# A two-layer mixer trunk: casts of weights behind the heads' high parts, numerators of two heads back to back, head 0's low part on VectorE, and a SwiGLU that starts with 256 features of gate and up in one bank

## The chip, the cores and the metric

The kernel runs on one core of one Trainium2 chip. The metric is device time in microseconds (us) of one execution. TensorE is called PE, VectorE DVE, ScalarE ACT, GpSimd POOL, and SyncE, which issues the loads, SP. L153 is line 153 of the kernel; the changed kernel is some lines shorter, so its L152 is the same line.

## The reference

The input is 256 tokens of 1024 features. Two layers follow each other, each with a token mixer, a SwiGLU channel mixer and a gated embedding:

```python
for i in range(2):
    y = gmlp_mixer(x, ...) if i == 0 else mlstm_mixer(x, ...)
    x = layer_norm(ALPHA * x + y, ln1_g[i], ln1_b[i])
    x = layer_norm(ALPHA * x + swiglu(x, ffn_w_gate[i], ffn_w_up[i], ffn_w_down[i]), ln2_g[i], ln2_b[i])
    gate = sigmoid(x @ ple_w_gate[i] + ple_b_gate[i])
    x = x + gate * (p[i] @ ple_w_proj[i])

def swiglu(x, w_gate, w_up, w_down):          # 2816 features = 22 blocks of 128
    return (silu(x @ w_gate) * (x @ w_up)) @ w_down
```

The mLSTM mixer of layer 1 has four heads of 512 features. A head's score matrix, times a decay, gives a numerator (scores times values) and a denominator (row sums); the quotient is normalised per head, a skip term is added, the result is multiplied by silu(z) and projected down. Everything is float32.

## The kernel before

**Arithmetic.** Each float32 operand of a matmul is split into a high part (a cast to fp32r, on ACT) and a low part (a subtraction, on DVE; `split`, L153). A product is three matmuls: high by high, low by high, high by low.

**Weights.** Weights arrive as float32 tiles of 128 x 1024 (512 KB) into four raw buffers through SP's queue, in the order of `weight_plan`; `EARLY` moves some of them ahead in that order, and those of `WIDE` live in a pool of large tiles of their own ("b8"). `weight(...)` is called where a tile is used and keeps up to 8 tiles loaded and up to 4 split ahead of the use. A raw buffer is free again, and the next load can start, when the tile's cast and its subtraction are done. `behind["cast"]` names instructions after which the casts called for from then on are put in the order. A scheduler sets the order of each engine's instructions from dependencies and program order; ACT's order in the heads follows the program.

**PSUM.** Matmul results go to eight banks, four in pool A (accumulators, heads' numerators) and four in pool B.

**SwiGLU** (`channel_mixer`). The tokens are two tiles of 128. First, `first(t)` computes 512 features of gate and then 512 of up for tile t with the tokens stationary: 8 chunks of 128 inputs times three products, 24 matmuls of 512 columns each for gate and for up (L286 and L287 high and low weights, L289 the input's low part). That makes 96 matmuls for both tiles. Between gate and up of tile 0 stands `transpose_x(1)` (L326), which turns token tile 1 of the normalised input (xn) into feature-major order, splits it and so makes tile 1's part of xs. The layer norm before it runs on DVE (L335 to L344). The products silu(gate) times up (hn) are token-major; four PE transposes per tile (L562) turn them into the first four feature blocks. The other 18 blocks come from `gate_up(f)`, which keeps the weights stationary: for gate and up each 8 matmuls of 512 columns (L260, the high and low part of xs side by side) and 8 of 256 (L264). The down projection (`Down`, L240 to L242) takes 12 matmuls of 512 columns per feature block and runs two blocks behind.

**Heads** (`mlstm`). For each head, DVE adds a mask to gate sums (gm, L909), ACT takes three exponentials (e, L911 to L913), DVE multiplies the scores by them (sc, L917), ACT casts the high part (phi, L153), and POOL subtracts the low part (plo, L153). Meanwhile PE computes blocks of z (zps, 24 matmuls of 256 columns, L245 to L247). `pv_block(h)` then computes head h's numerators for both token tiles (num, L937 to L939, two banks of pool A) and denominators (pd, L943 and L944). DVE takes the statistics (dn to hrs, L949 to L961), POOL a power (L962), DVE the factors (hrs and nb, L963 and L965), and ACT writes the normalised rows (hn, L967), which frees the two banks. `h_block(h)` transposes hn on PE (L976), and DVE and ACT finish and split the four feature blocks of the head (y, L980, L981; h, L153). Afterwards `acc = Down(NI)` takes the four banks of pool A for the down projection. The order before, on PE, is: numerators of head 0, z block 12, head 1, z 13, head 2, z 14, transposes of head 0, head 3, z 15, transposes of head 1, accumulation.

Of the kernel before, what the change touches and what calls it, by code (L numbers as in the profile page):

```python
# [14 lines left out]
P = 128  # L15
D = 1024
S = 256
# [29 lines left out]

WIDE = {(n, l, k) for l in range(2) for n, m in (("g", 4), ("u", 2), ("pg", 6)) for k in range(m)}  # L50
EARLY = {("wo", 17 + k): ("g", 0, k) for k in range(4)}
EARLY |= {("mo", 8 + 2 * k): ("g", 1, k) for k in range(3)}
EARLY |= {("d", l, 10 + k): ("pg", l, k) for l in range(2) for k in range(6)}


def down_blocks(f):

    return range(4) if f == 3 + LAG else [f - LAG] if f > 3 + LAG else []

# [2 lines left out]

def stationary(key):

    return key[0] in ("u", "xm") and len(key) == 2 or key[0] in ("g", "u", "z") and key[-1] >= 4


def paired(key):  # L70

    return key[0] in ("g", "u") and len(key) == 3 and key[-1] >= 4 or key[0] == "u" and len(key) == 2


def weight_plan(a):
# [3 lines left out]
    def add(key, ap):  # L79
        plan.append((key, ap))  # L80
# [11 lines left out]

    def ffn(l):
        add(("pj", l, 0), a["ple_proj"][l, 0])
        for n in ("g", "u"):
            for kp in range(4):
                add((n, l, kp), a["ffn_" + n][l, kp])
        for f in range(4, NF + LAG):
            for n in ("g", "u") if f < NF else ():
                add((n, l, f), a["ffn_" + n][l, f])  # L100
            for e in down_blocks(f):
                add(("d", l, e), a["ffn_d"][l, e])
        add(("pj", l, 1), a["ple_proj"][l, 1])
        for k in range(KD):
            add(("pg", l, k), a["ple_gate"][l, k])
# [28 lines left out]
def trunk(ctx, tc, a, out):  # L134
# [10 lines left out]
    def tl(tag, shape, dt=F32, name="t"):  # L145
        return sb.tile(shape, dt, tag=tag, name=name, bufs=BUFS[tag])

    def bank(which, shape, name="ps"):
        return (psA if which == "A" else psB).tile(shape, F32, tag=which, name=name)
# [58 lines left out]
    def weight(*key, casts=None):  # L208
        at["use"] = max(at["use"], place[key])
        ahead(LOAD_AHEAD, CAST_AHEAD if casts is None else casts)  # L210
        at["use"] = max(at["use"], place[key] + 1)
        return wt.pop(place[key])
# [304 lines left out]
    def channel_mixer(l, acc, last, hook=None):  # L517
# [19 lines left out]

        fw = {}  # L540

        def first(t, between=lambda: None):
            ps = {}
            for n in ("g", "u"):
                if t == 0:
                    fw[n] = [weight(n, l, kp) for kp in range(4)]
                ps[n] = bank("B", [P, 512], "first")
                tok_from_x(ps[n], t, fw[n])
                if n == "g":
                    between()  # L550
            h = tl("m2", [P, 512], name="hn")
            act.activation(h, ps["g"], AF.Silu)
            dve.tensor_tensor(h, h, ps["u"], ALU.mult)
            return h

        hn = [first(0, lambda: transpose_x(1)), first(1)]
        hs = {e: tl("h", [P, 2, S], F32R, "h") for e in range(4)}

        def transpose_h(t):
            tp = bank("B", [P, 4, P], "tp")  # L560
            for e in range(4):
                pe.transpose(tp[:, e, :], hn[t][:, e * P:(e + 1) * P], ident)  # L562
            for e in range(4):
                split(hs[e][:, 0, TOK[t]], hs[e][:, 1, TOK[t]], tp[:, e, :])

        def gate_up(f):
# [20 lines left out]

        transpose_h(0)
        rows = []
        for f in range(4, NF + LAG):  # L590
            if f < NF:
                gate_up(f)
            if f == 4:
                transpose_h(1)
                acc = Down(NF)
            for e in down_blocks(f):
                acc.add(e, hs.pop(e), weight("d", l, e, casts=1 if f >= NF else None))
            if f in (8, 10, 12):

                with issue_after([at["dma"]]):  # L600
                    rows.append(load_row(a[("ln2_g", "ln2_b", "ple_b")[f // 2 - 4]][l]))
            if f == 14 and hook:
                hook()
            if f == NF - 1:
                ahead(LOAD_AHEAD, LAG + 1)
# [96 lines left out]
    def mlstm(embed1):  # L702
# [156 lines left out]
        with tc.manual_schedule(engines={mybir.EngineType.Activation}):  # L859
# [43 lines left out]
            for h in range(NH):  # L903
# [13 lines left out]
                dve.scalar_tensor_tensor(p, p, DH ** -0.5, e, ALU.mult, ALU.mult)  # L917
                hi = tl("h", [P, 384], F32R, "phi")
                lo = tl("h", [P, 384], F32R, "plo")
                split(hi, lo, p, sub=pool)  # L920
                ph.append((hi, lo))
            z_copy(*z)
            act.activation(sz[1][:, 0:4, :], sz[1][:, 0:4, :], AF.Silu)

# [58 lines left out]
                    split(hs[f][:, 0, :], hs[f][:, 1, :], y)  # L983

        for h in range(NH):
            if h == NH - 1:
                ahead(LOAD_AHEAD, 4)
            pv_block(h)
            z_act(*z_mm(12 + h))
            if h == NH - 2:  # L990
                h_block(0)
        acc = Down(NI)
        begin = []
        for h in range(NH):
# [21 lines left out]
def lay_out(inputs):  # L1016
# [26 lines left out]
    def part(w):  # L1043
# [11 lines left out]
        "gm_wsT": i["gm_w_s"][0].transpose(2, 0, 1).reshape(P, NG * P),  # L1055
        "gm_bs": i["gm_b_s"][0].reshape(-1),
        "gm_gb": np.stack([i["gm_ln_g"][0], i["gm_ln_b"][0]], 1).reshape(NU, P, 2).transpose(1, 0, 2),
        "ffn_g": np.stack([mixed(w) for w in i["ffn_w_gate"]]),
        "ffn_u": np.stack([mixed(w) for w in i["ffn_w_up"]]),
        "ffn_d": i["ffn_w_down"].reshape(2, NF, P, D),  # L1060
        "ple_proj": i["ple_w_proj"].reshape(2, 2, P, 2, 512).transpose(0, 3, 2, 1, 4).reshape(2, 2, P, D),
        "ple_gate": i["ple_w_gate"].reshape(2, KD, P, D),
# [41 lines left out]
```

## Time and profile before

| what | value |
| --- | --- |
| median of 3 runs | 825.27 us (825.23 to 825.81) |
| profiled execution | 825.63 us |
| its span | 823.9 us |
| PE busy | 816.9 us, 99% of the span, 4520 matmuls |
| DVE busy | 614.3 us, 75% |
| ACT busy | 470.9 us, 57% |
| POOL busy | 149.6 us, 18% |
| granted clock of PE | 1.0 |
| data moved | 155.52 MB, mean 189 GB/s |

A row of a timeline gives the start in us, the duration in us, engine, line, operation, output and inputs by the program's names, and how many like it follow each other. In brackets stands the idle time of the engine before it and what ended that. Matmuls are pipelined: the duration of one reaches over the start of the next, so PE's time for one is read from start to start. The span leaves out 1.7 us around the profiled execution.

### The profile page before, as it was taken

What the parts mean: (1) busy time and instruction counts of PE and PEld (TensorE: products, weight loads), DVE (VectorE), ACT (ScalarE), POOL (GpSimd) and SP (SyncE); (2) the same over time, 40 slices, a digit from 0 to 9 for tenths busy, and PEclk for the clock granted to TensorE, in tenths of its full rate; (3) what the DMA queues carried; (4) which work ended last, traced back from release to release, by engine and by line L of the source; (5) the groups of instructions that cost most, each with busy time, mean ns of one, the idle gap of its engine ahead of it and who ended that gap; (6) DMA issues with size and microseconds to landing.
All of it is one profiled execution on the core that took longest, in us unless ns stands there. A gap on an engine that the chain in (4) does not pass through costs nothing.

```text
span 823.9 us, 12407 instructions
## 1 busy us (share of the span) xinstructions
PE 816.9 (99%) x4520; PEld 708.0 (86%) x4520; DVE 614.3 (75%) x982; ACT 470.9 (57%) x820; POOL 149.6 (18%) x209
## 2 busy tenths in 40 slices
PE   9999999999999999999999999999999999999997
PEld 6888888888888888888889999988888888888886
DVE  6757998678956567586878998889885656776674
ACT  6656666565535556475256788776444555665522
POOL 1020643342000000700001677330000000000000
PEclk9999999999999999999999999999999999999999
DMA  8895447567176678677144355454626667886501
GB/s 287 283 337 182 153 159 225 179 194 243 67 260 202 192 225 281 201 229 252 38 146 156 135 162 161 146 177 147 215 90 224 196 199 228 269 264 212 179 1 51
DMA packets 44997, 155.52 MB, mean 189 GB/s; under 512 B 5256, under 2 KB 6024, under 8 KB 44936
## 3 DMA queue, kind: packets, MB, share of 16 engines
q1 hardware_dynamic: 44792, 154.60, 57.6%
q8 instruction: 35, 0.57, 0.3%
q14 instruction: 26, 0.21, 0.1%
q10 hardware_dynamic: 144, 0.13, 0.0%
HBM read 153.67 MB, written 1.05 MB: 188 GB/s over the span
## 4 chain that ended last, share of the span: by engine, by line
PE 96%; DVE 1%; ACT 1%; DMA 1%; issue 0%; POOL 0%; SPq 0%; DVEq 0%; ACTq 0%
PE acc L240 9%; PE acc L241 9%; PE acc L242 9%; PE pu L260 8%; PE pg L260 8%; PE ups L260 5%; PE pg L264 4%; PE pu L264 4%; PE ups L264 3%; PE vps L242 2%; PE vps L240 2%; PE vps L241 2%; PE xmps L245 2%; PE xmps L247 2%; PE xmps L246 2%; PE gate L289 2%
## 5 line engine op out<-in xcount | busy, mean ns | idle before, releaser
L153 DVE TENSOR_TENSOR w<-raw,w 128x1024 fp32r<-128x1024 f32 (+1 forms) x275 | 333.2, 1219 | 74.7 <-ACT w L153 73.1
L153 ACT CAST w<-raw 128x1024 fp32r<-128x1024 f32 (+1 forms) x275 | 284.9, 1046 | 120.6 <-PE acc L242 25.7
L240 PE MATMUL acc<-w,h 128*128 128x512 f32 x336 | 133.0, 396 | 0.2 <-ACT hn L967 0.2
L241 PE MATMUL acc<-w,h 128*128 128x512 f32 x336 | 131.3, 391 | 0.0
L242 PE MATMUL acc<-w,h 128*128 128x512 f32 x336 | 131.0, 390 | 0.0
L242 PEld LDWEIGHTS acc<-w,h 128*128 128x128 f32 x336 | 63.1, 188 | 13.9
L240 PEld LDWEIGHTS acc<-w,h 128*128 128x128 f32 x336 | 63.1, 188 | 12.1 <-ACT hn L967 0.6
L241 PEld LDWEIGHTS acc<-w,h 128*128 128x128 f32 x336 | 63.1, 188 | 11.2 <-DVE h L153 0.2
L260 PE MATMUL pg<-xs,w 128*128 128x512 f32 x288 | 71.6, 391 | 0.0
L260 PE MATMUL pu<-xs,w 128*128 128x512 f32 x288 | 71.5, 390 | 0.0
L260 PEld LDWEIGHTS pg<-xs,w 128*128 128x128 f32 x288 | 53.8, 188 | 11.0
L260 PEld LDWEIGHTS pu<-xs,w 128*128 128x128 f32 x288 | 53.8, 188 | 11.0
L319 POOL TENSOR_TENSOR rs<-ve,mhalf 128x1 f32<-128x1 f32 x8 | 7.6, 956 | 295.9 <-DVE ve L318 291.3
L271 ACT COPY s<-pg 128x256 f32<-128x256 f32 x36 | 13.4, 372 | 69.7 <-PE pg L264 69.7
L260 PE MATMUL ups<-xs,w 128*128 128x512 f32 x192 | 47.9, 391 | 0.0
L272 DVE TENSOR_TENSOR s<-s,pg 128x256 f32<-128x256 f32 x36 | 15.1, 421 | 42.8 <-ACT s L271 42.7
L260 PEld LDWEIGHTS ups<-xs,w 128*128 128x128 f32 x192 | 35.7, 188 | 7.2
L264 PEld LDWEIGHTS pg<-xs,w 128*128 128x128 f32 x288 | 38.9, 188 | 3.1
L264 PE MATMUL pg<-xs,w 128*128 128x256 f32 x288 | 39.5, 280 | 0.0
L264 PE MATMUL pu<-xs,w 128*128 128x256 f32 x288 | 39.4, 279 | 0.0
L264 PEld LDWEIGHTS pu<-xs,w 128*128 128x128 f32 x288 | 36.5, 188 | 0.3
L245 PE MATMUL xmps<-xs,w 128*128 128x256 f32 x128 | 36.3, 284 | 0.0
(252 smaller groups left out, 1635.7 us busy)
## 6 DMA issues: line engine op xcount, KB each, us to landing
raw<-in_ffn_g SPq DMA_DIRECT2D x44, 512.0 KB, 4.4
raw<-in_ffn_u SPq DMA_DIRECT2D x44, 512.0 KB, 4.6
raw<-in_ffn_d SPq DMA_DIRECT2D x44, 512.0 KB, 4.3
raw<-in_gm_u SPq DMA_DIRECT2D x24, 512.0 KB, 3.5
raw<-in_gm_wo SPq DMA_DIRECT2D x24, 512.0 KB, 3.4
raw<-in_gm_v SPq DMA_DIRECT2D x21, 512.0 KB, 5.2
raw<-in_ple_gate SPq DMA_DIRECT2D x16, 512.0 KB, 4.5
raw<-in_ml_z SPq DMA_DIRECT2D x16, 512.0 KB, 3.8
```

What stands on the lines that cost most here:

```text
L153: return dve.tensor_copy(hi, src) if fast else act.copy(hi, src), sub.tensor_tensor(lo, src, hi.bitcast(F32), ALU.subtract)
L240: pe.matmul(ps, lh, w[:, 0, c], start=start, stop=False)
L241: pe.matmul(ps, ll, w[:, 0, c], start=False, stop=False)
L242: pe.matmul(ps, lh, w[:, 1, c], start=False, stop=stop)
L245: pe.matmul(ps, w[:, 0, c], h, start=start, stop=False)
L246: pe.matmul(ps, w[:, 0, c], l, start=False, stop=False)
L247: pe.matmul(ps, w[:, 1, c], h, start=False, stop=stop)
L260: pe.matmul(ps, w[:, 0, k * P:(k + 1) * P], xs[:, k], start=k == 0, stop=False)
L264: pe.matmul(ps[:, 0], w[:, 1, k * P:(k + 1) * P], xh[:, k, :], start=False, stop=k == KD - 1)
L271: act.copy(o, ps[:, 1])
L272: dve.tensor_tensor(o, o, ps[:, 0], ALU.add)
L289: pe.matmul(ps, xl[:, k, TOK[t]], w[:, 0, c], start=False, stop=k == KD - 1)
```

## The change

There are four edits.

1. **SwiGLU.** `first(t)` now computes 256 features of gate and the same 256 of up side by side in one bank of 512 columns, from four weight tiles "f" that hold both: 24 matmuls per token tile, 48 in all. The loop over `gate_up` starts at feature block 2 and makes 20 blocks. `transpose_x(1)` stands in tile 0 after the 16 matmuls with the input's high part. Two transposes per tile turn hn, which has 256 columns. In each layer 44 weight tiles are read, as before.
2. **Weights ahead.** The four "f" tiles of each layer are moved ahead and live in large tiles (before: four gate tiles in layer 0 and three in layer 1 were moved ahead, and four gate and two up tiles of each layer were in large tiles).
3. **Casts behind the high parts.** After the last head's high part is cast, `behind["cast"]` names that cast, so casts of weights called for later stand behind it. Head 0's low part is subtracted on DVE, those of the others on POOL as before.
4. **Heads in pairs.** The order on PE is: numerators of head 0, z 12, head 1, z 13, head 2, head 3, z 14, transposes of head 0, z 15, transposes of head 1, accumulation. The call that looks ahead in the weights moves behind the transposes of head 0.

```diff
-WIDE = {(n, l, k) for l in range(2) for n, m in (("g", 4), ("u", 2), ("pg", 6)) for k in range(m)}
-EARLY = {("wo", 17 + k): ("g", 0, k) for k in range(4)}
-EARLY |= {("mo", 8 + 2 * k): ("g", 1, k) for k in range(3)}
+WIDE = {(n, l, k) for l in range(2) for n, m in (("f", 4), ("pg", 6)) for k in range(m)}
+EARLY = {("wo", 17 + k): ("f", 0, k) for k in range(4)}
+EARLY |= {("mo", 8 + 2 * k): ("f", 1, k) for k in range(4)}
...
-    return range(4) if f == 3 + LAG else [f - LAG] if f > 3 + LAG else []
+    return range(2) if f == 1 + LAG else [f - LAG] if f > 1 + LAG else []
...
-        for n in ("g", "u"):
-            for kp in range(4):
-                add((n, l, kp), a["ffn_" + n][l, kp])
-        for f in range(4, NF + LAG):
+        for kp in range(4):
+            add(("f", l, kp), a["ffn_f"][l, kp])
+        for f in range(2, NF + LAG):
...
+        def first(t, before=(None, None)):
+            if t == 0:
+                fw.extend(weight("f", l, kp) for kp in range(4))
+            ps = bank("B", [P, 512], "first")
+            tok_from_x(ps, t, fw, before)
+            h = tl("m2", [P, 256], name="hn")
+            act.activation(h, ps[:, :256], AF.Silu)
+            dve.tensor_tensor(h, h, ps[:, 256:], ALU.mult)
             return h
-        hn = [first(0, lambda: transpose_x(1)), first(1)]
-        hs = {e: tl("h", [P, 2, S], F32R, "h") for e in range(4)}
+        hn = [first(0, (0, lambda: transpose_x(1))), first(1)]
+        hs = {e: tl("h", [P, 2, S], F32R, "h") for e in range(2)}
...
-        for f in range(4, NF + LAG):
+        for f in range(2, NF + LAG):
             if f < NF:
                 gate_up(f)
-            if f == 4:
+            if f == 2:
                 transpose_h(1)
...
-                split(hi, lo, p, sub=pool)
+                end = split(hi, lo, p, sub=pool if h else dve)
                 ph.append((hi, lo))
+            behind["cast"] = end[:1]
...
         for h in range(NH):
-            if h == NH - 1:
-                ahead(LOAD_AHEAD, 4)
             pv_block(h)
-            z_act(*z_mm(12 + h))
-            if h == NH - 2:
-                h_block(0)
+            if h < 2:
+                z_act(*z_mm(12 + h))
+        z_act(*z_mm(14))
+        h_block(0)
+        ahead(LOAD_AHEAD, 4)
+        z_act(*z_mm(15))
```

The order of instructions shows what the edits move. On PE at the first features of layer 0, the rows before around the transposes of token tile 1 (xn_80):

```order
741 L286 MATMUL first<-w,xs 128x512
742 L287 MATMUL first<-w,xs 128x512
743 L289 MATMUL first<-w,xs 128x512 x8
744 L326 MATMUL tp<-ident,xn_80 128x128 x8
745 L286 MATMUL first<-w,xs 128x512
```

and now:

```order
741 L285 MATMUL first<-w,xs 128x512
742 L286 MATMUL first<-w,xs 128x512
743 L325 MATMUL tp<-ident,xn_80 128x128 x8
744 L288 MATMUL first<-w,xs 128x512 x8
745 L285 MATMUL first<-w,xs 128x512
```

The eight transposes stood behind tile 0's 24 gate matmuls and stand now behind its first 16; row 745 began tile 0's up features and now begins tile 1.

On ACT in the heads, from head 1's last exponential to the switch of the function table, the rows before:

```order
486 L913 ACTIVATE e<-gm,cols 128x128
487 L915 ACTIVATE cols<-cols 128x8
488 L153 CAST w<-raw 128x1024
489 L153 CAST phi<-sc 128x384
490 L911 ACTIVATE e<-gm,cols 128x128
491 L912 ACTIVATE e<-gb,cols 128x128
492 L913 ACTIVATE e<-gm,cols 128x128
493 L153 CAST w<-raw 128x1024
494 L153 CAST phi<-sc 128x384
```

and now, from head 3's high part on:

```order
502 L152 CAST phi<-sc 128x384
503 L749 COPY sz<-zps 128x256
504 L746 ACT_TABLE_LOAD
505 L746 ACTIVATE sz<-zps 128x256
506 L921 ACTIVATE sz<-sz 128x1024
507 L965 ACTIVATE hn<-num,nb,hrs 128x512 x2
508 L152 CAST w<-raw 128x1024
509 L965 ACTIVATE hn<-num,nb,hrs 128x512 x2
510 L746 ACTIVATE sz<-zps 128x256
511 L152 CAST w<-raw 128x1024 x4
512 L746 ACTIVATE sz<-zps 128x256
513 L965 ACTIVATE hn<-num,nb,hrs 128x512 x2
```

The casts of weights between the heads' steps are gone from there; the first comes behind head 0's normalised rows (507), and four stand together between z 13 (510) and z 14 (512), ahead of head 2's rows (513).

On DVE at the same place, the rows before, from the mask additions of the heads to the second product of scores:

```order
562 L909 TENSOR_TENSOR gm<-gb,cmask 128x256 x2
563 L153 TENSOR_TENSOR w<-raw,w 128x1024
564 L917 SCALAR_TENSOR_TENSOR sc<-sc,e 128x384
565 L153 TENSOR_TENSOR w<-raw,w 128x1024
566 L909 TENSOR_TENSOR gm<-gb,cmask 128x256
```

and now, from head 0's on:

```order
569 L904 TENSOR_TENSOR gm<-gb,cmask 128x256 x2
570 L912 SCALAR_TENSOR_TENSOR sc<-sc,e 128x384
571 L904 TENSOR_TENSOR gm<-gb,cmask 128x256
572 L152 TENSOR_TENSOR plo<-sc,phi 128x384
573 L912 SCALAR_TENSOR_TENSOR sc<-sc,e 128x384
```

The subtractions of weights have left the stretch, and head 0's low part stands between the third mask addition and the second product of scores.

More of the change, by code (lines that the diff above doesn't have):

```diff
@@ L45 @@
 Z_AFTER_XM = {1: 4, 5: 5, 10: 6, 15: 7}
-WIDE = {(n, l, k) for l in range(2) for n, m in (("g", 4), ("u", 2), ("pg", 6)) for k in range(m)}
-EARLY = {("wo", 17 + k): ("g", 0, k) for k in range(4)}
-EARLY |= {("mo", 8 + 2 * k): ("g", 1, k) for k in range(3)}
+WIDE = {(n, l, k) for l in range(2) for n, m in (("f", 4), ("pg", 6)) for k in range(m)}
+EARLY = {("wo", 17 + k): ("f", 0, k) for k in range(4)}
+EARLY |= {("mo", 8 + 2 * k): ("f", 1, k) for k in range(4)}
 EARLY |= {("d", l, 10 + k): ("pg", l, k) for l in range(2) for k in range(6)}
 def down_blocks(f):
-    return range(4) if f == 3 + LAG else [f - LAG] if f > 3 + LAG else []
+    return range(2) if f == 1 + LAG else [f - LAG] if f > 1 + LAG else []
 ASIDE = 56
 def stationary(key):
-    return key[0] in ("u", "xm") and len(key) == 2 or key[0] in ("g", "u", "z") and key[-1] >= 4
+    return key[0] in ("g", "u", "xm") or key[0] == "z" and key[-1] >= 4
 def paired(key):
-    return key[0] in ("g", "u") and len(key) == 3 and key[-1] >= 4 or key[0] == "u" and len(key) == 2
+    return key[0] in ("g", "u")
 def weight_plan(a):
@@ L94, in ffn @@
         add(("pj", l, 0), a["ple_proj"][l, 0])
-        for n in ("g", "u"):
-            for kp in range(4):
-                add((n, l, kp), a["ffn_" + n][l, kp])
-        for f in range(4, NF + LAG):
+        for kp in range(4):
+            add(("f", l, kp), a["ffn_f"][l, kp])
+        for f in range(2, NF + LAG):
             for n in ("g", "u") if f < NF else ():
-                add((n, l, f), a["ffn_" + n][l, f])
+                add((n, l, f), a["ffn_" + n][l, f - 2])
             for e in down_blocks(f):
@@ L536, in channel_mixer @@
         boundary(0, g1, b1)
[L540 to L553, printed above, removed]
-            return h
-        hn = [first(0, lambda: transpose_x(1)), first(1)]
-        hs = {e: tl("h", [P, 2, S], F32R, "h") for e in range(4)}
+        fw = []
+        def first(t, before=(None, None)):
[6 more added lines that the diff above has]
+            dve.tensor_tensor(h, h, ps[:, 256:], ALU.mult)
+            return h
+        hn = [first(0, (0, lambda: transpose_x(1))), first(1)]
+        hs = {e: tl("h", [P, 2, S], F32R, "h") for e in range(2)}
         def transpose_h(t):
-            tp = bank("B", [P, 4, P], "tp")
-            for e in range(4):
+            tp = bank("B", [P, 2, P], "tp")
+            for e in range(2):
                 pe.transpose(tp[:, e, :], hn[t][:, e * P:(e + 1) * P], ident)
-            for e in range(4):
+            for e in range(2):
                 split(hs[e][:, 0, TOK[t]], hs[e][:, 1, TOK[t]], tp[:, e, :])
@@ L1057, in lay_out @@
         "gm_gb": np.stack([i["gm_ln_g"][0], i["gm_ln_b"][0]], 1).reshape(NU, P, 2).transpose(1, 0, 2),
-        "ffn_g": np.stack([mixed(w) for w in i["ffn_w_gate"]]),
-        "ffn_u": np.stack([mixed(w) for w in i["ffn_w_up"]]),
+        "ffn_f": np.stack([
+            tok(np.concatenate([g[:, :256], u[:, :256]], 1))[0] for g, u in zip(i["ffn_w_gate"], i["ffn_w_up"])
+        ]),
+        "ffn_g": np.stack([feat(w[:, 256:]) for w in i["ffn_w_gate"]]),
+        "ffn_u": np.stack([feat(w[:, 256:]) for w in i["ffn_w_up"]]),
         "ffn_d": i["ffn_w_down"].reshape(2, NF, P, D),
```

## The prediction

> **What bounds the kernel now.** I read the page first, then the list of waits on TensorE (PE), then the chain that ended last. On the page, busy time and the chain by engine:
>
> ```profile
> PE 816.9 (99%) x4520; PEld 708.0 (86%) x4520; DVE 614.3 (75%) x982; ACT 470.9 (57%) x820; POOL 149.6 (18%) x209
> ...
> PE 96%; DVE 1%; ACT 1%; DMA 1%; issue 0%; POOL 0%; SPq 0%; DVEq 0%; ACTq 0%
> ```
>
> The waits of PE, each group with its total, its count and its longest:
>
> ```profile
> PE warm L357 <- DVE warm L354: 1.2, 1, 1.2
> PE vps L422 <- ACT w L382: 0.6, 1, 0.6
> PE num L939 <- POOL plo L153: 0.5, 1, 0.5
> PE vps L422 <- ACT xs L378: 0.2, 1, 0.2
> PE acc L240 <- ACT hn L967: 0.2, 1, 0.2
> ```
>
> PE is busy for 816.9 of 823.9 us and 96% of the chain is its own work. Behind the start it waits twice in the whole program: for head 0's low part, and for head 3's normalised rows. So time can be won only by fewer or shorter PE instructions and at these two waits, and it can be lost only where another engine, now hidden, becomes later than PE. The profiled execution took 825.63 us, 0.36 above the median of 825.27; I sum changes on it and take them from the median.
>
> **SwiGLU, each layer.** The timeline of PE, from the start of the first features in layer 0 to the first block, and one later turn of the loop:
>
> ```profile
> 219.52 0.39 PE L286 MATMUL first<-w,xs 128*128 128x512 f32 x1
> ...
> 223.15 1.98 PE L289 MATMUL first<-w,xs 128*128 128x512 f32 x8
> 224.97 1.04 PE L326 MATMUL tp<-ident,xn 128*128 128x128 f32 x8
> 225.76 0.47 PE L286 MATMUL first<-w,xs 128*128 128x512 f32 x1
> ...
> 242.21 0.60 PE L562 MATMUL tp<-ident,hn 128*128 128x128 f32 x4
> 242.56 1.18 PE L260 MATMUL pg<-xs,w 128*128 128x512 f32 x4
> ...
> 265.08 1.29 PE L260 MATMUL pg<-xs,w 128*128 128x512 f32 x5
> ...
> 273.32 0.84 PE L260 MATMUL pg<-xs,w 128*128 128x512 f32 x3
> ```
>
> A 512-column matmul takes (223.15 − 219.52)/16 = 0.227 us of PE (0.2275 over the eight from 223.15 to 224.97). The change drops 48 of the 96 matmuls of the first features: 48 × 0.2275 = 10.92 us. It adds two more turns of gate and up. One loop turn is 273.32 − 265.08 = 8.24 us and holds, beside one such block, 12 matmuls of 512 columns for the down projection (2.73), so the block is 5.51; the down matmuls stay as many. A block is 16 matmuls of 512 columns and 16 of 256, and the chain has eight of the latter:
>
> ```profile
> 246.50 0.94 PE pg L264 x8
> ```
>
> That is 0.1175 each, so the widths alone give 16 × 0.2275 + 16 × 0.1175 = 5.52, the same within the rounding. I take 5.51, as the loop has it: two blocks cost 11.02, a loss of 0.10 per layer (0.12 with 5.52), since two narrow matmuls cost a little more than a wide one. The Trainium skill, TensorE: Matmul & The Clock Gate, section Back-to-back issue gap, gives the isolated gap as columns over 2.4 GHz plus about 2.5 ns, 216 and 109 ns, so smaller matmuls pay the fixed part twice, which speaks against this change. By it the loss would be an estimated 0.04 us per layer instead of 0.10; the rows above are slower at both widths, and the measurement decides.
>
> The gain is in the transposes of the products: four took 242.56 − 242.21 = 0.35 us, two should take half. Two token tiles drop 2 × 0.175 = 0.35 us. Per layer −0.35 + 0.10 = −0.25; two layers **−0.50** (−0.46 with the dearer block).
>
> The same weight bytes are loaded and split. The two first gate and up tiles of the loop now must be ready 48 matmuls sooner, but they are also taken at the place in the plan where the second half of the old first weights stood; those were split here, right behind the layer norm:
>
> ```profile
> 222.37 0.75 DVE L344 SCALAR_TENSOR_TENSOR xn<-xn,rs,row 128x512 f32<-128x512 f32 x1
> 223.04 4.63 DVE L153 TENSOR_TENSOR w<-raw,w 128x1024 fp32r<-128x1024 f32 x4
> 227.59 1.28 DVE L153 TENSOR_TENSOR xs<-tp,xs 128x512 fp32r<-128x512 f32 x2
> ```
>
> Four subtractions done by 227.67; the loop would start at 242.56 − 10.92 − 0.35 or about 231.3, so 3.6 us cover them. I cost this at nothing. Token tile 1's transposes move from 24 to 16 matmuls behind the start: 219.52 + 16 × 0.2275 = 223.16, and the layer norm that they read ends at 223.12. The second half alone needs that end, four transposes (0.40) later. Its low part is needed 24 matmuls after the transposes' end at 223.95, at 229.4, and is there at 228.87 in the row above. In layer 1 the margin is larger:
>
> ```profile
> 611.83 0.75 DVE L344 SCALAR_TENSOR_TENSOR xn<-xn,rs,row 128x512 f32<-128x512 f32 x1
> ...
> 609.70 0.40 PE L286 MATMUL first<-w,xs 128*128 128x512 f32 x1
> ```
>
> The norm ends at 612.58, and 16 matmuls end at 613.35. I take 0; if the cover of 0.4 to 0.8 is gone it costs what the norm is late (rival below).
>
> **Head 0's low part on VectorE (DVE).** Timelines of DVE, ScalarE (ACT), GpSimd (POOL) and PE there:
>
> ```profile
> 533.34 0.54 DVE L917 SCALAR_TENSOR_TENSOR sc<-sc,e 128x384 f32<-128x384 f32 x1
> 533.91 0.51 ACT L153 CAST phi<-sc 128x384 fp32r<-128x384 f32 x1 [0.65 <-DVE sc L917]
> 534.47 1.20 DVE L153 TENSOR_TENSOR w<-raw,w 128x1024 fp32r<-128x1024 f32 x1
> 534.50 2.04 POOL L153 TENSOR_TENSOR plo<-sc,phi 128x384 fp32r<-128x384 f32 x1 [11.40 <-ACT phi L153]
> 535.74 0.40 PE L938 MATMUL num<-vn,phi 128*128 128x512 f32 x1
> 536.60 0.50 PE L939 MATMUL num<-vn,plo 128*128 128x512 f32 x1 [0.47 <-POOL plo L153]
> 536.94 0.39 PE L937 MATMUL num<-vn,phi 128*128 128x512 f32 x1
> ...
> 542.07 1.29 DVE L957 BATCH_NORM_STATS2 hst<-num 128x6 f32<-128x512 f32 x2
> 542.51 1.02 POOL L153 TENSOR_TENSOR plo<-sc,phi 128x384 fp32r<-128x384 f32 x1 [1.04 <-ACT phi L153]
> ```
>
> From 535.74 PE needs 0.86 to its next start and 0.34 to the one behind, against 0.23 each: 0.74 us are lost, more than the 0.47 that the list names. The high part is there at 534.42. A DVE operation with 384 elements takes 0.54 (the first row), so the low part is there at about 535.0, while PE asks for it at 535.97. The weight subtraction that holds DVE at 534.47 is deferred by the same change. So the wait goes: **−0.74** (bounds −0.74, and 0 if it is late by as much as now).
>
> **Heads in pairs, casts deferred.** The casts of four weight tiles, and with them their subtractions, leave the stretch from 532 to 541 and follow the last head's high part. Head 3's products follow head 2's at once. PE issues the same matmuls. What can change is the second wait:
>
> ```profile
> 553.71 0.48 PE L937 MATMUL num<-vn,phi 128*128 128x512 f32 x1
> 556.44 0.36 PE L245 MATMUL zps<-xs,w 128*128 128x256 f32 x1
> ...
> 559.36 1.04 PE L976 MATMUL tp<-ident,hn 128*128 128x128 f32 x8
> 560.15 0.48 PE L240 MATMUL acc<-w,h 128*128 128x512 f32 x1
> ...
> 564.78 0.39 PE L242 MATMUL acc<-w,h 128*128 128x512 f32 x1
> 565.35 0.50 PE L240 MATMUL acc<-w,h 128*128 128x512 f32 x1 [0.18 <-ACT hn L967]
> 565.68 0.39 PE L241 MATMUL acc<-w,h 128*128 128x512 f32 x1
> ```
>
> ```profile
> 564.51 1.45 ACT L967 ACTIVATE hn<-num,nb,hrs 128x512 f32<-128x512 f32 x2 [0.75 <-DVE nb L965]
> ...
> 600.15 1.37 DVE L335 SCALAR_TENSOR_TENSOR xn<-xn,acc 128x512 f32<-128x512 f32 x2 [3.81 <-PE acc L242]
> ```
>
> The down projection's second accumulators reuse head 3's numerator banks, so PE waits until head 3 is normalised: 565.35 − 564.78 is 0.57 and the next step 0.33, against 0.23 each, 0.45 us lost. Head 3's products now take 2.73 us (553.71 to 556.44), the z block behind them 2.92, and the transposes 0.79. In pairs these products end one z block and one set of transposes earlier, and 0.74 with the gain above: near 552.0 instead of 556.44. With today's 8.1 us from there to the normalisation it starts at 560.1; two of the deferred subtractions (1.20 each) now stand in that DVE chain, some of them in idle time, so I estimate 560.3 to 560.8. The accumulation starts at 560.15 − 0.74 = 559.4; by the order the banks are asked for after 6 accumulations and 5 transposes, 1.37 + 0.5, at 561.3, and the first normalisation then ends at 561.1 to 561.6. A wait of about the old size stays: I take **0**, between −0.45 and +1.7. The upper end is where both deferred subtractions land whole on that path (2.4), less the 0.7 that the middle of my estimate already holds.
>
> The four subtractions, 4 × 1.2 = 4.8, must fit in before the layer norm at 600.15, where DVE now idles 3.81, beside smaller gaps. They also hold four raw buffers, so the next loads wait some 14 us; four weight tiles ahead, taken at 12 matmuls (2.73) each, cover them.
>
> **Sum:** −0.50 − 0.74 + 0 = −1.24: 824.4 for such an execution, 825.27 − 1.24 = **824.0** for the median. About 0.2%, 1.65 us, is what a measurement of this kernel can tell from no change; the forecast is inside it.
>
> **The rivals.** *Both waits go.* If the pairs make head 3 early by 0.5 more than I think, all of 0.50 + 0.74 + 0.45 = 1.69 is won: 823.6, just beyond 0.2%. For it: the products end over 4 us earlier. Against: the deferred subtractions sit in that chain. Nothing in the list of waits allows more.
>
> *DVE falls behind, slower.* All deferred subtractions queue on DVE between 547 and 600, ahead of the heads' chains and the split of the down projection's rows. POOL's part of each chain suffers too: the low part beside a weight subtraction took 2.04, beside the statistics 1.02, so such company costs 1.0, twice here for heads 2 and 3. 4.8 − 3.8 of idle + 2.0 is 3.0 us that PE would wait, at head 3's banks and at the norm: 824.0 + 3.0 = 827.0. It decides from 2.9 us of lag on. Against it: smaller idle stretches of DVE (0.5 to 0.8 before several of its chain steps) and PE's pace, which lets DVE catch up. The Trainium skill, SBUF — State Buffer, section Who interferes with whom, says that a DVE operation with two inputs in SBUF and a GpSimd operation that reads SBUF exclude each other for the whole instruction. The two rows of the low part agree: 1.17 us of the 2.04 lie beside the subtraction.
>
> *The earlier transposes wait.* If other DVE work slips ahead of token tile 1's norm or of its low part by one weight subtraction (1.2) in one or both layers, 0.4 to 0.8 of each are covered: up to 0.6 a layer, 1.2 in all, and the gain is spent: 825.2.
>
> *The low part's wait does not go.* If it stands behind the mask additions on DVE until after 536.7, its −0.74 is missing: 824.8.
>
> **How the numbers follow.** Forecast 0.52; both waits go 0.20; earlier transposes wait 0.12; the low part stays late 0.08; DVE behind 0.08. Faster by over 0.2% is the second alone, 0.20; slower the last alone, 0.08; the rest, 0.72, lies within. The range begins at 823.3, the full gain and 0.3 for steps at which PE's pace may be better than the rows say, and goes to 826.2, the upper bound of head 3's wait (824.0 + 1.7) and half a microsecond of lag at the norm; the worst case lies outside.
>
> **What would show it.** Right: the wait on the low part gone from the list; 48 matmuls of first features and 20 turns per layer; the span down by 1.0 to 1.5; a wait of 0.1 to 0.6 on head 3's rows. Wrong: PE waiting for token tile 1 at 223 or 613; waits for weights or rows between 550 and 600; a block that costs other than 5.51; the layer norm of layer 1 starting later than 599.

## The result and the profile after

The changed kernel takes 827.59 us (median of 7 runs, 826.72 to 828.79); the kernel before, run beside it, 825.45 (825.16 to 825.86). The ratio is 1.0027, with a 95% interval of 1.0018 to 1.0036: slower, by about 2.1 us. The forecast was 824.0, at most 826.2. Two executions among the experiments below, one with the casts behind head 2 and one with the products of all heads on POOL, ran at granted clocks of 0.56 and 0.75 (1367.59 and 1013.27 us), and the medians and ratios leave them out.

The profiled execution took 827.36 us with a span of 825.6, and 825.63 with 823.9 before. On its page, busy times and the chain that ended last:

```profile
PE 817.8 (99%) x4544; PEld 708.7 (86%) x4544; DVE 617.3 (75%) x991; ACT 472.6 (57%) x828; POOL 149.5 (18%) x208
...
PE 94%; DVE 3%; DMA 2%; ACT 1%; issue 1%; POOL 0%; SPq 0%; DVEq 0%; ACTq 0%
```

PE's share of the chain fell from 96% to 94%, and DVE and the DMAs came in. The waits of PE in the changed kernel:

```profile
PE warm L356 <- DVE warm L353: 1.2, 1, 1.2
PE acc L239 <- ACT w L152: 1.2, 1, 1.2
PE acc L241 <- DVE w L152: 0.5, 1, 0.5
PE vps L421 <- ACT w L381: 0.2, 1, 0.2
```

Both old waits are gone from the list (low part of head 0, rows of head 3). In their place PE waits for the high part and for the low part of a weight (w) in a down projection (acc). The timeline of PE puts them at the end of the mLSTM mixer:

```profile
596.72 0.39 PE L241 MATMUL acc<-w,h 128*128 128x512 f32 x1
597.20 0.50 PE L239 MATMUL acc<-w,h 128*128 128x512 f32 x1
597.53 0.40 PE L240 MATMUL acc<-w,h 128*128 128x512 f32 x1
598.46 0.50 PE L241 MATMUL acc<-w,h 128*128 128x512 f32 x1 [0.53 <-DVE w L152]
598.79 0.40 PE L239 MATMUL acc<-w,h 128*128 128x512 f32 x1
...
599.26 0.40 PE L241 MATMUL acc<-w,h 128*128 128x512 f32 x1
600.82 0.50 PE L239 MATMUL acc<-w,h 128*128 128x512 f32 x1 [1.17 <-ACT w L152]
601.16 0.39 PE L240 MATMUL acc<-w,h 128*128 128x512 f32 x1
...
601.63 0.39 PE L240 MATMUL acc<-w,h 128*128 128x512 f32 x1
602.09 0.72 PE L241 MATMUL acc<-w,h 128*128 128x512 f32 x2
602.65 0.40 PE L239 MATMUL acc<-w,h 128*128 128x512 f32 x1
```

From start to start a matmul costs 0.23. The steps of 0.48, 0.33, 0.93, 0.33, 1.56, 0.34 and 0.46, and the 0.56 of the two matmuls from 602.09 to 602.65, hold some 2.95 us above that. The list of waits shows 1.7 of it; as before the change, the full price is only seen from start to start.

The chain of waits up to there, in order of time:

```profile
587.39 0.76 DVE h L152 x2
588.15 0.67 DVE y L979 x2
588.82 0.84 DVE w L152
...
589.88 0.75 DVE h L152 x2
590.63 3.42 DVE w L152 x3
...
594.07 5.56 DMA raw<-in_ml_wo
...
599.73 1.05 ACT w L152
...
600.80 1.24 DVE w L152
...
602.09 0.72 PE acc L241 x2
```

Read it backwards. PE waits for the subtraction of the last down-projection weight, that for its cast, the cast for its load (5.56), and the load for a raw buffer, which three subtractions on DVE free one after the other up to 594.07. Ahead of these DVE works, from 587.39 on without a break, on the rows of head 3 (y, h). So DVE decides here, a stretch earlier than PE waits. The last load also takes 5.56, where a load of these weights took 4.3 in the median: from 591 to 603 the DMAs are busy for a share of 0.90, and for 0.65 in the kernel before. What this crowding adds was not tested by itself.

How far the weights are behind is seen on DVE. The kernel before splits its fifth down-projection weight here:

```profile
558.32 1.21 DVE L153 TENSOR_TENSOR w<-raw,w 128x1024 fp32r<-128x1024 f32 x1
```

and the changed kernel its second and third here:

```profile
554.16 1.23 DVE L152 TENSOR_TENSOR w<-raw,w 128x1024 fp32r<-128x1024 f32 x1
...
561.36 1.22 DVE L152 TENSOR_TENSOR w<-raw,w 128x1024 fp32r<-128x1024 f32 x1
```

At 561 us it is three tiles behind. Counted by the ends of these subtractions it is two behind at 571.3, and again three at 580.2 and at 594.5. Busy time of DVE by stretch, before (stretch, its length, busy time and instructions of DVE, clock, DMA share, GB/s):

```profile
531.00:546.00 15.00, 13.75 (x32) 1.00 0.71 257
546.00:561.00 15.00, 13.05 (x42) 1.00 0.26 76
561.00:576.00 15.00, 13.89 (x31) 1.00 0.53 177
576.00:591.00 15.00, 13.38 (x25) 1.00 0.61 204
```

and after:

```profile
531.00:546.00 15.00, 10.85 (x34) 1.00 0.31 101
546.00:561.00 15.00, 12.32 (x38) 1.00 0.44 141
561.00:576.00 15.00, 13.80 (x29) 1.00 0.49 161
576.00:591.00 15.00, 14.05 (x26) 1.00 0.56 191
```

Between 531 and 546 DVE does 2.9 us less, since the four subtractions have left, and the DMAs move 101 GB/s instead of 257, since the raw buffers stay full. By 561 DVE has done 3.6 us less than before (23.17 for 26.80). From 561 to 591 it is 92 to 94% busy, against 89 to 93% before, and makes up 0.6 of them: there is almost no room for the missing work.

### The profile page after: what moved, and what is told of

It reads as the page before. It is cut to its first block, busy times and chain, and to the rows that moved or that the text cites. A ratio compares the mean times of both kernels' runs of the same rounds, so it can differ in the third digit from the quotient of the medians.

```text
span 825.6 us, 12481 instructions
## 1 busy us (share of the span) xinstructions
PE 817.8 (99%) x4544; PEld 708.7 (86%) x4544; DVE 617.3 (75%) x991; ACT 472.6 (57%) x828; POOL 149.5 (18%) x208
## 4 chain that ended last, share of the span: by engine, by line
PE 94%; DVE 3%; DMA 2%; ACT 1%; issue 1%; POOL 0%; SPq 0%; DVEq 0%; ACTq 0%
PE pu L259 9%; PE pg L259 9%; PE acc L239 8%; PE acc L241 8%; PE acc L240 8%; PE ups L259 5%; PE pg L263 5%; PE pu L263 5%; PE ups L263 3%; PE vps L241 2%; PE vps L239 2%; PE vps L240 2%; PE xmps L244 2%; PE xmps L246 2%; PE xmps L245 2%; PE gate L288 2%
## 5 line engine op out<-in xcount | busy, mean ns | idle before, releaser
L259 PE MATMUL pg<-xs,w 128*128 128x512 f32 x320 | 79.5, 391 | 0.0
L259 PE MATMUL pu<-xs,w 128*128 128x512 f32 x320 | 79.4, 390 | 0.0
L259 PEld LDWEIGHTS pu<-xs,w 128*128 128x128 f32 x320 | 59.8, 188 | 12.3
L259 PEld LDWEIGHTS pg<-xs,w 128*128 128x128 f32 x320 | 59.8, 188 | 12.3
L271 DVE TENSOR_TENSOR s<-s,pg 128x256 f32<-128x256 f32 x40 | 16.8, 421 | 66.0 <-ACT s L270 66.0
L263 PEld LDWEIGHTS pg<-xs,w 128*128 128x128 f32 x320 | 43.2, 188 | 3.4
L263 PE MATMUL pg<-xs,w 128*128 128x256 f32 x320 | 43.9, 280 | 0.0
L263 PE MATMUL pu<-xs,w 128*128 128x256 f32 x320 | 43.7, 279 | 0.0
L263 PEld LDWEIGHTS pu<-xs,w 128*128 128x128 f32 x320 | 40.6, 188 | 0.3
```

Source lines behind the costliest of these rows:

```text
L259: pe.matmul(ps, w[:, 0, k * P:(k + 1) * P], xs[:, k], start=k == 0, stop=False)
L263: pe.matmul(ps[:, 0], w[:, 1, k * P:(k + 1) * P], xh[:, k, :], start=False, stop=k == KD - 1)
L271: dve.tensor_tensor(o, o, ps[:, 0], ALU.add)
```

## The experiments

All medians below stand beside the kernel before on the same chip, 825.36 to 825.63. "At the last weights" is PE's time above 0.23 a step there in the one profiled execution of each kernel, summed as above. The runs of one kernel spread over 0.7 to 3.1 us, and the intervals are about 0.7 to 1.1 us to either side, so two medians that differ by less than 1 us are not told apart.

| kernel | median | ratio, 95% interval | at the last weights |
| --- | --- | --- | --- |
| changed kernel | 827.59 | 1.0018 to 1.0036 | 2.95 |
| e1, three tiles ahead | 827.91 | 1.0017 to 1.0039 | 3.3 |
| e2, no deferral | 826.11 | 1.0003 to 1.0020 | 0 |
| e4, SwiGLU alone | 825.08 | 0.9987 to 1.0004 | 0 |
| e5, heads alone | 828.65 | 1.0024 to 1.0051 | 1.5 |
| e7, SwiGLU and low part | 827.62 | 1.0013 to 1.0036 | 0 |
| e8, no pairs | 829.18 | 1.0034 to 1.0061 | 2.6 |
| e10, casts behind head 1 | 825.08 | 0.9988 to 1.0005 | 0.5 |
| e10, casts behind head 2 | 825.90 | 0.9995 to 1.0013 | 1.3 |
| e11, smaller pools | 828.56 | 1.0025 to 1.0051 | 2.5 |
| e11, and a fifth raw buffer | 828.79 | 1.0023 to 1.0048 | 2.0 |
| e12, behind head 1, products of heads 0, 1 on POOL | 825.37 | 0.9991 to 1.0009 | 0 |
| e13, pairs, no deferral, low part on POOL | 824.90 | 0.9984 to 1.0001 | 0 |
| e14, products of heads 2, 3 on POOL | 825.47 | 0.9989 to 1.0007 | 0.5 |
| e14, products of all heads on POOL | 826.33 | 0.9999 to 1.0017 | 1.7 |
| e16, pairs, behind head 0, low part on POOL | 825.04 | 0.9984 to 1.0002 | 0.7 |
| e16, and products of heads 2, 3 on POOL | 824.42 | 0.9979 to 0.9996 | 0 |
| e17, kernel before, products of heads 2, 3 on POOL | 825.52 | 0.9993 to 1.0011 | 0 |

**Which edit.** Theory 1 was that the deferred casts stop the loads; the rival, theory 2, that the fourth SwiGLU tile, moved ahead of the last down-projection weight, delays that weight.

```diff
-EARLY |= {("mo", 8 + 2 * k): ("f", 1, k) for k in range(4)}
+EARLY |= {("mo", 8 + 2 * k): ("f", 1, k) for k in range(3)}
```

> The changed kernel (827.59 us) with three instead of four of layer 1's first SwiGLU tiles moved ahead among the mixer's down-projection weights, so that no foreign tile stands between the last two of those weights. Theory 1 (the deferred casts hold the raw buffers, loading stops for some 12 us, and the last down-projection weights come late): the pause stays, so PE still waits at those weights, at most the one load's step of 1.1 us less: 826.5 to 827.6. Theory 2 (the fourth tile takes a turn of load, cast and subtraction ahead of the last weight): most of the 2.8 us of waits go: 824.6 to 825.2. If both are needed: about 826.

827.91: nothing gained, 3.3 us at the last weights; the median is 0.3 above even theory 1's range. Theory 2 falls.

```diff
-            behind["cast"] = end[:1]
```

> The changed kernel without the deferral: casts of weights are no longer put behind the last head's high part; four tiles are moved ahead, heads in pairs, and head 0's low part on VectorE stay. Theory 1: the pause in the loads goes and with it all 2.8 us of waits at the last down-projection weights: 824.6 to 825.2 (some of the 0.74 of the low part may come back, since a weight subtraction stands before it on VectorE again). Theory 2: the fourth tile still stands ahead of the last weight, the waits stay: 826.8 to 827.8. If both are needed: about 825.5 to 826.

826.11, and no wait at the last weights, as theory 1 has it for that place. But 1.5 us are won, not 2.8, since another wait comes in. In the profile without the deferral, PE's only listed wait after 540:

```profile
PE num L934 <- ACT hn L964: 1.1, 1, 1.1
```

Head 3's numerators now follow head 2's with four matmuls of z between them, and take the banks of head 1, whose rows are late when the four subtractions run among the heads' chains. The pairs bring a wait of their own where the subtractions are not deferred.

```diff
-                end = split(hi, lo, p, sub=pool if h else dve)
+                split(hi, lo, p, sub=pool)
-            behind["cast"] = end[:1]
...
         for h in range(NH):
+            if h == NH - 1:
+                ahead(LOAD_AHEAD, 4)
             pv_block(h)
-            if h < 2:
-                z_act(*z_mm(12 + h))
-        z_act(*z_mm(14))
-        h_block(0)
-        ahead(LOAD_AHEAD, 4)
-        z_act(*z_mm(15))
+            z_act(*z_mm(12 + h))
+            if h == NH - 2:
+                h_block(0)
```

> The changed kernel with the heads as they were before (low part on GpSimd, casts between the heads, heads one by one); only the SwiGLU and the four tiles moved ahead are new. Theory 1: no pause in the loads, so only the SwiGLU's gain of 0.5 shows: 824.8 to 825.1. Theory 2: the waits at the last weights are there, 825.45 - 0.5 + 2.8, about 826.5 to 827.8.

825.08, theory 1's figure: the SwiGLU, with its four tiles ahead, wins some 0.3 (an interval that holds no change) and costs nothing at the last weights.

The new heads in the kernel before (edits 3 and 4 without 1 and 2):

```diff
-                split(hi, lo, p, sub=pool)
+                end = split(hi, lo, p, sub=pool if h else dve)
...
+            behind["cast"] = end[:1]
...
-            if h == NH - 1:
-                ahead(LOAD_AHEAD, 4)
             pv_block(h)
-            z_act(*z_mm(12 + h))
-            if h == NH - 2:
-                h_block(0)
+            if h < 2:
+                z_act(*z_mm(12 + h))
+        z_act(*z_mm(14))
+        h_block(0)
+        ahead(LOAD_AHEAD, 4)
+        z_act(*z_mm(15))
```

> The kernel before with the new heads alone (low part of head 0 on VectorE, casts behind the high parts, pairs); its SwiGLU is the old one and three tiles are moved ahead. Theory 1: the pause in the loads is there, 825.45 - 0.74 + about 2.8, 826.5 to 827.5. Theory 2: no fourth tile, so only the gain of 0.74 shows: 824.5 to 824.9.

828.65: the loss is in the heads. The median is 1.15 above theory 1's range and 1.06 above the changed kernel, whose interval overlaps this one; that the SwiGLU makes the loss smaller is thus likely, not shown. There is 1.5 us at the last weights, and 1.2 more in waits at layer 1's SwiGLU.

The changed kernel with the old order of the heads alone, the second half of the diff of e4:

```diff
+            if h == NH - 1:
+                ahead(LOAD_AHEAD, 4)
             pv_block(h)
-            if h < 2:
-                z_act(*z_mm(12 + h))
-        z_act(*z_mm(14))
-        h_block(0)
-        ahead(LOAD_AHEAD, 4)
-        z_act(*z_mm(15))
+            z_act(*z_mm(12 + h))
+            if h == NH - 2:
+                h_block(0)
```

> The changed kernel with the heads one by one as before; the deferral of the casts behind the last high part and the low part on VectorE stay. Theory 1 (the deferral alone holds the raw buffers and stops the loads for some 12 us): the waits at the last down-projection weights stay, 826.8 to 828. Theory 3 (the pairs are needed for the loss, because they crowd VectorE's chain): no such waits, 824.3 to 825.

829.18, 2.6 us at the last weights: the deferral costs this without the pairs too, and theory 3 falls. Another 1.9 stand at head 3's rows; the median is 1.2 above theory 1's range. For the same without the line `behind["cast"] = end[:1]`:

> The SwiGLU and head 0's low part on VectorE, without the deferral and with the heads one by one as before. By the terms of the forecast: 825.4 - 0.5 - 0.74 = 824.2 if the low part's wait goes whole; 824.5 to 824.9 if a weight subtraction (1.2) still stands ahead of it on VectorE and leaves part of the 0.74. Both theories of the loss expect no wait at the last down-projection weights here, so this tells only what the two gains are worth without the loss.

827.62, a miss of 3 us: the low part on DVE, which takes 0.7 off PE in the heads, makes the kernel slower than the SwiGLU alone (825.08). On PE:

```profile
563.79 0.39 PE L241 MATMUL acc<-w,h 128*128 128x512 f32 x1
566.31 0.51 PE L239 MATMUL acc<-w,h 128*128 128x512 f32 x1 [2.14 <-ACT hn L962]
```

The wait is 2.3, where the SwiGLU alone has 0.7. PE reaches head 3's banks 0.86 earlier than there (563.79 for 564.65), and head 3's rows begin 0.71 later (565.48 for 564.77). DVE, busy for 89 and 87% of the two stretches from 531 to 561, has 0.54 more to do ahead of them, and the order of its instructions differs too: a weight subtraction at 548.63 now stands inside head 1's chain, where it followed behind it at 549.46. Which of the two delays the rows was not separated. What PE won in this stretch came back as a wait, with interest; the two profiled executions differ by 1.5, the medians by 2.5. So four kernels stand in a square, each difference good to about 1 us. The deferral costs 1.5 with pairs (826.11 to 827.59) and 1.6 without (827.62 to 829.18). The pairs win 1.5 without the deferral and 1.6 with it.

**The dose.** The casts behind head 1's high part (and, with `h == 2`, behind head 2's):

```diff
-            behind["cast"] = end[:1]
+                if h == 1:
+                    behind["cast"] = end[:1]
```

> The changed kernel with the casts put behind head 1's high part instead of head 3's, so that four casts wait some 3 us instead of some 12. Theory 1 with its dose: the raw buffers come free near 538 to 542, loading stops for 3 to 5 us instead of 12, and the waits at the last weights fall from 2.8 to 0.5 or less; what is left is head 3's numerators waiting for head 1's rows (1.3 without any deferral): 824.6 to 825.6. If the loss had nothing to do with how long the casts wait: 827 to 828.

> The same with the casts behind head 2's high part: the wait of the casts is some 6 us. Theory 1 with its dose: loading stops for 5 to 8 us, waits at the last weights between those of the run behind head 1's high part and the 2.8 of the changed kernel, 0.3 to 1.5: 824.8 to 826.3. If the loss had nothing to do with how long the casts wait: 827 to 828.

825.08 and 825.90, within both expectations. The time at the last weights goes with the delay of the casts: 0 without deferral, 0.5 behind head 1, 1.3 behind head 2, 2.95 behind head 3. These are single executions, and the order holds among kernels with head 0's low part on DVE: with it on POOL, casts behind head 0 already show 0.7 (e16 below).

**Buffers or VectorE.** What cannot be made up: loads, for want of raw buffers (theory 1), or subtractions, for want of time on DVE (theory 4)? Memory has room for a fifth raw buffer if three other pools shrink, so the shrunk pools alone are the control.

```diff
-"raw": 4, "w": 6, "b8": 8, "row": 3, "h": HOLD + 5, "m2": 6, "s": 6, "c": 8, "cf": 3
+"raw": 4, "w": 6, "b8": 8, "row": 3, "h": HOLD + 5, "m2": 6, "s": 5, "c": 7, "cf": 2
```

> Control for the fifth raw buffer: the changed kernel with the same smaller pools (scratch tiles 6 to 5, small tiles 8 to 7, 384-element tiles 3 to 2) and still four raw buffers. All theories: as the changed kernel, 827 to 828.5, or a little more if a smaller pool makes someone wait.

```diff
-"raw": 4, "w": 6, "b8": 8, "row": 3, "h": HOLD + 5, "m2": 6, "s": 5, "c": 7, "cf": 2
+"raw": 5, "w": 6, "b8": 8, "row": 3, "h": HOLD + 5, "m2": 6, "s": 5, "c": 7, "cf": 2
```

> The changed kernel with a fifth raw buffer, for which three scratch pools are one tile smaller; the casts are deferred as in the changed kernel. Theory 1 (the raw buffers held by the deferred casts stop the loads): one more weight tile is loaded ahead of the pause and every later one is one tile, 2.7 us of PE's use, earlier, so most of the 2.8 to 3.0 us at the last weights goes: 2.0 to 3.0 below the control. Theory 4 (the deferred subtractions themselves are late, VectorE has no time for them): the fifth buffer changes nothing, within 0.5 of the control.

828.56 and 828.79: the fifth buffer does not win the 2 to 3 us of theory 1. A load more is issued ahead of the pause, but the waits are still there, 2.0 for 2.5. A gain of 1 us or less is not excluded: the two profiled executions take 828.85 and 827.80. Theory 1, as I had it, falls: the held buffers are a link of the chain, not most of the cost.

Then the reverse, with buffers, loads and deferral as they are and less work on DVE:

```diff
-                    dve.tensor_tensor(y, y, sz[f // 8][:, f % 8, :], ALU.mult)
+                    (pool if h > 1 else dve).tensor_tensor(y, y, sz[f // 8][:, f % 8, :], ALU.mult)
```

> The changed kernel with the products with silu(z) of heads 2 and 3 on GpSimd instead of VectorE: 8 x 0.42, 3.4 us less on VectorE between 563 and 590; buffers, loads and deferral as in the changed kernel. Theory 4 (the deferred subtractions land where VectorE is full, so what it idles before is lost): the 2.8 to 3.0 us of waits at the last down-projection weights fall to 1.0 or less, 825 to 826. Theory 1 (the raw buffers were held, and the loads cannot catch up whatever VectorE does): the waits stay, 827 to 828.

825.47, 2.1 us less than the changed kernel. Its waits of PE after 540:

```profile
PE acc L239 <- ACT hn L965: 0.4, 1, 0.4
PE acc L241 <- DVE w L152: 0.2, 1, 0.2
```

The waits at the last weights are 0.5 instead of 2.95, with the same deferral, as theory 4 has it. The kernel before with the same edit:

> Control: the kernel before with the products of heads 2 and 3 on GpSimd. It has no wait at the last weights, only the 0.45 at head 3's rows. Theory 4: little to win, 825.0 to 825.6. If the relief were a gain by itself, whatever the deferral: about 2 us, 823.3 to 823.8.

825.52, no change: the relief is worth nothing by itself here, and 2.1 us where the deferral has put DVE behind. With `pool.tensor_tensor` for all heads:

> The same with the products of all four heads on GpSimd, 6.7 us less on VectorE from 555 to 590. Theory 4: no wait at the last weights, and the 0.8 at head 3's rows goes too, 824 to 825.3. Theory 1: 827 to 828. If GpSimd's products are late themselves, PE waits for the split rows instead, and both theories would see more.

826.33, outside the ranges of both theories, with 1.7 at the last weights: more relief did not help more. Its profile shows one reason:

```profile
574.30 1.23 DVE L152 TENSOR_TENSOR w<-raw,w 128x1024 fp32r<-128x1024 f32 x1 [2.14 <-ACT w L152]
```

In this kernel a weight subtraction stands ahead of head 2's rows in DVE's order, and DVE idles for 2.14 until the weight is loaded and cast. With heads 2 and 3 alone on POOL, DVE does head 2's rows in that time, and the subtraction follows at 573.91. So the order of DVE's work counts beside its amount. Whether this is the whole difference was not tested.

**Other mixtures.** Behind head 1, with the products of heads 0 and 1 on POOL (`pool if h < 2 else dve`):

> The kernel with the casts behind head 1's high part (825.08), and the products with silu(z) of heads 0 and 1 on GpSimd instead of VectorE (8 x 0.4 us less on VectorE). Theory 5 (VectorE is full from 531 to 566, so what PE wins in the heads comes back as waits for head 3's rows and the split rows): the 1.3 us of waits at 559 to 562 fall to 0.5 or less, 824.0 to 824.6. If VectorE is not the limit there: 824.8 to 825.5, or more, since GpSimd's operation is slower.

825.37: the waits near 560 fell to 0.6 in the profile, but the median did not follow, a miss. PE loses 0.5 there to token tile 1's norm at layer 1's SwiGLU (0.4 without this edit). The pairs without the deferral and with all low parts on POOL:

```diff
-                end = split(hi, lo, p, sub=pool if h else dve)
+                split(hi, lo, p, sub=pool)
-            behind["cast"] = end[:1]
```

> The SwiGLU and the pairs, without the deferral and with head 0's low part on GpSimd as before. Theory 5: head 0's low part makes PE wait 0.7 as before, VectorE has 0.5 less to do, and head 3's numerators wait for head 1's rows: 825.2 to 826.2, no slower than the same with the low part on VectorE (826.11). If the low part on VectorE were a gain by itself: 826.5 to 827.

824.90, better than expected and 1.2 less than with the low part on DVE (826.11): PE waits for head 0's low part again, but the wait at head 1's rows falls from 1.4 to 0.5. With the casts behind head 0's high part, the low part still on POOL:

```diff
-                end = split(hi, lo, p, sub=pool if h else dve)
+                end = split(hi, lo, p, sub=pool)
-            behind["cast"] = end[:1]
+                if h == 0:
+                    behind["cast"] = end[:1]
```

> SwiGLU and pairs, the casts behind head 0's high part, head 0's low part on GpSimd. No weight subtraction runs beside that low part, so it should take 1.0 instead of 2.05 and end before PE asks for it: the wait of 0.74 goes. Theory 4: VectorE idles about 1.2 us there and no more, little of which is missed later: 824.9 - 0.74 + 0 to 0.6, 824.1 to 824.8. If any deferral costs what the deepest costs: 826 or more.

825.04, just above its expectation, with 0.7 at the last weights. Head 0's low part without this deferral (the run before) and with it:

```profile
533.76 2.04 POOL L152 TENSOR_TENSOR plo<-sc,phi 128x384 fp32r<-128x384 f32 x1 [11.39 <-ACT phi L152]
```

```profile
534.68 1.02 POOL L152 TENSOR_TENSOR plo<-sc,phi 128x384 fp32r<-128x384 f32 x1 [11.42 <-ACT phi L152]
```

With no weight subtraction beside it, it takes 1.02 instead of 2.04, and PE's wait of 0.74 is gone without any work moved to DVE. But 0.7 at the last weights stands in its place, and the median is that of the run before. And the same with the products of heads 2 and 3 on POOL:

> The same with the products of heads 2 and 3 on GpSimd. Theory 4: VectorE has time enough for all of it, no waits at the last weights and a shorter one at layer 1's first transposes: 823.7 to 824.6. If VectorE were not the limit: as the run without it, within 0.3.

824.42, ratio 0.9979 to 0.9996, the fastest here and below both kernels; its interval overlaps those of e4 and e13, so it is not shown to be faster than these. PE's only listed wait after 540 is one of 0.3 for the high part of some rows.

## Why the prediction was wrong

**SwiGLU: right.** The forecast was −0.25 a layer. From the first features to the second projection behind the loop (pps), the kernel before has

```profile
404.69 0.48 PE L240 MATMUL pps<-w,pt 128*128 128x512 f32 x1
...
794.96 0.48 PE L240 MATMUL pps<-w,pt 128*128 128x512 f32 x1
```

and the changed kernel

```profile
219.20 0.40 PE L285 MATMUL first<-w,xs 128*128 128x512 f32 x1
222.85 1.03 PE L325 MATMUL tp<-ident,xn 128*128 128x128 f32 x8
...
404.09 0.48 PE L239 MATMUL pps<-w,pt 128*128 128x512 f32 x1
...
611.74 0.39 PE L285 MATMUL first<-w,xs 128*128 128x512 f32 x1
...
796.67 0.47 PE L239 MATMUL pps<-w,pt 128*128 128x512 f32 x1
```

Layer 0: 404.69 − 219.52 = 185.17 before, 404.09 − 219.20 = 184.89 after, −0.28. Layer 1: 794.96 − 609.70 = 185.26 before, 796.67 − 611.74 = 184.93 after, −0.33. Token tile 1's transposes start 3.65 behind the first features, as counted, and nobody waits for them; that rival did not happen here. It is not far: in e10 behind head 1 and in e12, where PE comes to layer 1's first features earlier, it loses 0.4 and 0.5 to this norm.

**Head 0's low part: right on PE.**

```profile
533.91 0.56 DVE L152 TENSOR_TENSOR plo<-sc,phi 128x384 fp32r<-128x384 f32 x1 [0.25 <-ACT phi L152]
...
535.18 0.40 PE L936 MATMUL num<-vn,phi 128*128 128x512 f32 x1
535.41 0.40 PE L937 MATMUL num<-vn,plo 128*128 128x512 f32 x1
```

DVE needs 0.56 (0.54 estimated), and PE's step is 0.23: the whole 0.74 is won there. The rival of a late low part did not happen. But e7 shows that this gain was not safe: without the deferral and the pairs it came back, with more, at head 3's rows.

**Pairs: size about right.** I took 0 for the wait on head 3's rows, "a wait of about the old size".

```profile
560.29 0.93 PE L974 MATMUL tp<-ident,hn 128*128 128x128 f32 x5
561.32 0.50 PE L239 MATMUL acc<-w,h 128*128 128x512 f32 x1
561.66 0.40 PE L240 MATMUL acc<-w,h 128*128 128x512 f32 x1
...
560.49 1.45 ACT L965 ACTIVATE hn<-num,nb,hrs 128x512 f32<-128x512 f32 x2
```

The normalisation starts at 560.49, inside the estimate of 560.3 to 560.8, with two deferred subtractions (552.28 and 554.16) ahead of it on DVE, as foreseen. From 560.29 to 561.66 PE takes 1.37 for five transposes (0.5) and one matmul (0.23): it loses 0.65 in place of 0.45.

**The deferral: the step that failed.** It was costed at nothing, and covered twice: the four subtractions "must fit in before the layer norm at 600.15, where DVE now idles 3.81, beside smaller gaps", and of the held buffers, "four weight tiles ahead, taken at 12 matmuls (2.73) each, cover them". It cost 2.95 at the last weights, and 1.5 to 1.6 net by the medians, for without it other waits come in. Neither cover is one. The 3.81 of idle lies at the end: in the kernel before, DVE's last weight subtraction before it runs from 595.12 to 596.35. It comes too late for work on which PE's last weights depend: behind a raw buffer that DVE frees there still follow a load (5.56 at the end), a cast and a subtraction. And the tiles ahead are no stock that lasts. DVE is 92 to 94% busy from 561 to 591, so three tiles of lag at 561 are still there when the last tile is asked for. The dose (0, 0.5, 1.3, 2.95), the fifth buffer that took 0.5 off the waits and nothing off the median, and the relief of DVE that removed 2.5 show this. The run with the products of all heads on POOL does not fit by the amount of work alone, and why the order of DVE's work turned out as it did there stays open.

The rival "DVE falls behind, slower" had this mechanism and a price of 3.0, 827.0; it got 0.08. Its place was wrong: PE loses its time neither at head 3's banks (0.65, about the old size) nor at the norm but at the last down-projection weights. That its price agrees with the 2.95 is luck: it was 4.8 less 3.8 of idle and plus 2.0 for POOL, and of POOL's part only 0.9 on one power is seen. What spoke against it in the prediction, that small gaps and PE's pace let DVE catch up, rested on no row. The busy time of DVE by stretch, 13.89 and 13.38 of 15 us, was there to be read before.

The sum of what was measured: −0.61 for the SwiGLU, −0.74, +0.20 (0.65 for 0.45) and +2.95 make +1.80; the two profiled executions differ by 827.36 − 825.63 = 1.73. That these agree so well is partly luck. The changed execution reached layer 0's first features 0.32 earlier (219.20 for 219.52), ahead of every matmul that the edits touch, and from layer 0's pps to layer 1's first features it lost 2.64 (207.65 for 205.01), 0.23 more than the three terms there.

## What to carry to other kernels

Before an edit defers work on an engine that is not the bottleneck, read that engine's busy time in the stretches behind, not its mean and not its idle time at the end: at 75% over the span, DVE had 5.9 us of idle time in the 60 from 531 to 591. Deferred work that feeds a chain of load, cast and subtraction shows up far later, at the last tile of the chain, so look there for the wait. And a gain on PE in a stretch that another engine paces can come back as a wait, as in e7; look for work to take off that engine too, as in e16 with the products on POOL.

## What the runs showed of the hardware

In these runs an operation on POOL that reads SBUF took longer where it began beside a weight subtraction on DVE, which has two inputs in SBUF. Head 0's low part took 2.04 to 2.05 in each kernel with the subtraction there, and 1.02 in both with it moved. The small power on POOL does so too: 0.71 to 0.80 elsewhere in the changed kernel, but beside a deferred subtraction,

```profile
552.44 1.60 POOL L960 TENSOR_TENSOR hrs<-hrs,mhalf 128x2 f32<-128x2 f32 x1 [5.88 <-DVE hrs L959]
```

This agrees with the Trainium skill, SBUF — State Buffer, section Who interferes with whom: the later of the two blocks until the first is done. The other order is in the traces as well: with the products of all heads on POOL, a weight subtraction that began at 567.80, behind a product on POOL (566.89, 1.59), took 1.76 instead of 1.22. So work moved from DVE to POOL is not free for DVE.
